# Interleaved first weight lists, a shorter layer-norm head and an epilogue inside the layer norm, in an eight-core decoder layer

## Chip, cores and metric

The kernel runs on all 8 cores of one Trainium2 chip (two dies of four cores), each core on 1024 tokens of its own; nothing is exchanged. The metric is device time in microseconds (us) of the slowest core. A program on all cores has a fast and a slow state: in many executions one die, or both, runs at a lower granted TensorE clock and the time grows by some per cent. Unless I say otherwise I compare executions in which no die was slowed ("fast"), or single dies at the full clock.

Ratios quoted as such are the mean time of one kernel's fast runs over the mean of the other's fast runs of the same rounds, so not quite the ratio of the medians or single times that I quote beside them.

## The reference

```python
D_MODEL, BATCH, SEQ, N_META = 4096, 4, 2048, 16
D_FF = 11008
def reference(x, meta_tokens, ...):
    h = concatenate([meta, x], axis=1)
    h = layer_norm(ALPHA * h + 0.5 * swiglu_ffn(h, ffn1...), ln1)
    h = layer_norm(ALPHA * h + hybrid_mixer(h, w_in, conv_w, pool_w, pool_scale, w_out), ln2)
    h = layer_norm(ALPHA * h + 0.5 * swiglu_ffn(h, ffn2...), ln3)
    return h[:, N_META:]
# layer_norm: mean and variance over the 4096 features, (x-mu)*rsqrt(var+1e-5)*g+b, in float32
# swiglu_ffn: silu(h Wg) * (h Wu), then Wd; hybrid_mixer: a projection to 8192 columns,
# a gated short convolution, four causal window means, an output projection
```

## The kernel before

Tokens lie along the free dimension, features along partitions, so the 4096 features are 32 chunks of 128. A core takes its tokens in two halves (528 columns, 16 of them a halo of earlier tokens, then 512). For each half it runs: prologue (load and transpose the input), FFN 1, layer norm, mixer, layer norm, FFN 2, layer norm, epilogue (transpose and store). `hacc` holds the residual in float32, `hb` the normalised activations in bf16.

Weights stream through a ring of five slots of 1 MB. One slot is one "unit": 16 chunks by 256 output columns, converted to bf16 on the way. A list of two units makes two banks of results in PSUM, where matmuls accumulate (four banks where the 528 columns are split in two):

```python
def mm_block(wv, col0, kchunks, rhs_fn, rhs_keys_fn, subs, b0):
    ...
    while k0 < nk_tot:
        nk = min(16, nk_tot - k0)
        slot = add_unit(wv, kchunks[0] + k0, nk, col0)     # DMA into ring[slot], waits until it is free
        ...                                                # fn: 16 x 2 matmuls (x nsub)
        reads = [("w", slot)]
        for kk in range(nk):
            reads += rhs_keys_fn(k0 + kk)                  # waits for all 16 chunks of hb
        P.op("pe", fn, reads=reads, writes=bkeys(b0, 2 * nsub))
```

The head of each layer norm, after ones-matmuls have summed over the partitions, and its loop:

```python
# ACT: mean = ps/D                        L349
# DVE: tmp = mean*mean                    L351
# DVE: tmp = ps2/D - tmp                  L353
# DVE: tmp = tmp + EPS                    L356
# ACT: tmp = Sqrt(tmp)                    L358
# DVE: rstd = 1/tmp                       L360
for c in range(NCH):
    # DVE: t1 = hacc[c] - mean            L366
    # DVE: t2 = t1 * rstd                 L368
    # not final: ACT hb[c], ACT hacc[c]   L376, L380
    # final:     ACT hacc[c]              L371
...
```

The epilogue came after that loop: for each block of 128 tokens, eight groups of four transposes, a copy of each group alternately on ACT and DVE into one of two staging buffers (16 KB in each partition), one 2 MB store. The prologue of the second half uses the same two buffers for its loads.

## Time and profile before

| | kernel before |
|---|---|
| first three timed runs | 9115.62, 9807.81, 10494.77 us (the first is fast) |
| profiled run, slowest core | 9118.2 us, clock 0.977, fast |
| PE busy | 8678.6 us, 95% |
| PE standing still | 440 us by subtraction; 394 us in the listed waits |

The lines themselves are in the prediction. Read them so: PE is the TensorE matmul row, ACT is ScalarE, DVE is VectorE, POOL issues the weight loads and SP the input loads and stores; a row of waits names the waiting engine and line, what it waited for, and then total us, number of waits and longest. A timeline row gives start, length, engine and line, output and inputs, count, and in brackets the idle time just before with what ended it. "PE ps L272 <- ACT hb L376" is the weight matmuls waiting for a chunk of `hb` that ACT writes at L376.

### The profile page before, as it was taken

Reading aid. Unit: us, or ns where it says so; the run is one execution under the profiler, and the core shown is the slowest. Engines: PE = TensorE matmul, PEld = TensorE weight load, DVE = VectorE, ACT = ScalarE, POOL = GpSimd, SP = SyncE. Lnnn points to the kernel's source line nnn. Section 1 sums busy time; section 2 is a strip of 40 time slices with the busy share of each in tenths; the row PEclk is TensorE's granted clock in tenths of the full one; section 3 lists DMA queues with packets and bytes.
Section 4 is the critical chain, followed back from the end, with each engine's and each line's share of the span. In section 5 each row is a group of like instructions: output and inputs, shape, how many; then the busy total and the mean of one; then the engine's idle time right before and its main releaser. Section 6 shows DMA issues by size and latency. Waiting matters only on the chain.

```text
span 9118.2 us, 110310 instructions; the slowest of 8 cores (9110.8 to 9118.2 us)
## 1 busy us (share of the span) xinstructions
PE 8678.6 (95%) x49081; PEld 4904.7 (54%) x49680; DVE 1259.2 (14%) x1482; ACT 646.0 (7%) x808; POOL 675.7 (7%) x1284
## 2 busy tenths in 40 slices
PE   8999999979989999999879999999799799999996
PEld 7888888867634444444444444444344344444443
DVE  1000000142130000000320000001412300000014
ACT  1000000020020000000120000000200200000002
POOL 0000000000000000000000000000000000000000
PEclk9999999989999999999989999999899899999998
DMA  8888888869878888898769898988698699998995
GB/s 156 147 145 148 144 150 146 145 104 154 146 126 140 150 155 153 151 154 151 138 152 154 150 155 150 155 152 149 111 159 146 115 152 151 154 153 150 155 150 111
DMA packets 187414, 1328.84 MB, mean 146 GB/s; under 512 B 20784, under 2 KB 21040, under 8 KB 47664
## 3 DMA queue, kind: packets, MB, share of 16 engines
q0 software_dynamic: 184320, 1287.73, 83.4%
q1 hardware_dynamic: 2624, 34.01, 1.1%
q8 instruction: 396, 6.49, 0.3%
q14 instruction: 74, 0.61, 0.0%
HBM read 2592.54 MB, written 16.78 MB: 286 GB/s over the span
## 4 chain that ended last, share of the span: by engine, by line
PE 94%; ACT 2%; DVE 2%; DMA 1%; issue 1%; DVEq 0%; ACTq 0%; SPq 0%
PE ps L272 93%; ACT hb L376 1%; DMA gy<-xin 1%; DVE scr L366 1%; ACT hacc L380 1%; PE ps L593 0%; DVE scr L368 0%; DMA y<-gy 0%; PE ps L339 0%; DVE scr L360 0%; PE ps L621 0%; DVE gy L630 0%; DVE scr L327 0%; ACT gy L627 0%; DVE scr L323 0%
## 5 line engine op out<-in xcount | busy, mean ns | idle before, releaser
L272 PE MATMUL ps<-hb,ring 128*128 128x512 bf16 (+1 forms) x32761 | 5702.1, 335 | 203.0 <-ACT hb L376 180.2
L272 PEld LDWEIGHTS ps<-hb,ring 128*128 128x128 bf16 x33152 | 3248.9, 98 | 2654.4 <-issue 203.2
L272 PE MATMUL ps<-gy,ring 128*128 128x512 bf16 (+1 forms) x15603 | 2838.8, 343 | 18.9 <-DVE gy L554 8.1
L272 PEld LDWEIGHTS ps<-gy,ring 128*128 128x128 bf16 x15808 | 1547.7, 98 | 1308.0 <-issue 14.5
L408 DVE TENSOR_TENSOR gy<-ps,scr 128x1024 bf16<-128x1024 f32 (+1 forms) x172 | 212.1, 1233 | 4587.9 <-PE ps L272 4587.9
L253 POOL DMA_DIRECT2D ring<-w_gu x688 | 363.2, 528 | 4687.9 <-PE ps L272 4641.3
L401 ACT ACTIVATE scr<-ps 128x1024 f32<-128x1024 f32 (+1 forms) x172 | 177.2, 1030 | 6149.2 <-PE ps L272 6149.1
L418 DVE SCALAR_TENSOR_TENSOR hacc<-ps,hacc 128x1024 f32<-128x1024 f32 (+1 forms) x192 | 236.8, 1233 | 1986.7 <-PE ps L272 1986.7
L253 POOL DMA_DIRECT2D ring<-w_d x384 | 202.6, 528 | 2250.9 <-PE ps L272 2216.5
L309 ACT ACTIVATE scr<-hacc 128x1024 f32<-128x1024 f32 (+1 forms) x96 | 101.9, 1062 | 1225.0 <-DVE hacc L418 775.0
L621 PE MATMUL ps<-identS,hacc 128*128 128x128 f32 x256 | 48.5, 345 | 103.2 <-ACT hacc L371 93.5
L368 DVE TENSOR_TENSOR scr<-scr 128x512 f32<-128x512 f32 (+1 forms) x192 | 133.5, 695 | 20.5 <-DVE scr L366 0.5
L253 POOL DMA_DIRECT2D ring<-w_in x128 | 67.5, 528 | 874.3 <-PE ps L272 865.2
L366 DVE TENSOR_TENSOR scr<-hacc,scr 128x512 f32<-128x512 f32 (+1 forms) x192 | 132.2, 688 | 0.6
L323 DVE TENSOR_TENSOR scr<-scr,hacc 128x512 f32<-128x512 f32 (+1 forms) x180 | 125.1, 695 | 21.2 <-DVE scr L323 1.4
L327 DVE TENSOR_TENSOR scr<-scr 128x512 f32<-128x512 f32 (+1 forms) x180 | 124.5, 691 | 9.4
L593 PE MATMUL ps<-identS,gy 128*128 128x128 f32 (+1 forms) x288 | 44.3, 330 | 73.7 <-DMA gy<-xin 73.6
L376 ACT ACTIVATE hb<-scr,vecsS 128x512 bf16<-128x512 f32 (+1 forms) x128 | 102.8, 803 | 20.8 <-DVE scr L368 20.7
L380 ACT ACTIVATE hacc<-scr,avecsS 128x512 f32<-128x512 f32 (+1 forms) x128 | 102.8, 803 | 0.0
L621 PEld LDWEIGHTS ps<-identS,hacc 128*128 128x128 f32 x256 | 37.6, 179 | 115.0 <-issue 114.5
L569 DVE TENSOR_TENSOR hacc<-ps,hacc 128x1024 f32<-128x1024 f32 x32 | 39.2, 1225 | 321.8 <-PE ps L272 321.8
L593 PEld LDWEIGHTS ps<-identS,gy 128*128 128x128 f32 (+1 forms) x288 | 43.0, 180 | 75.0 <-issue 75.0
(42 smaller groups left out, 584.1 us busy)
## 6 DMA issues: line engine op xcount, KB each, us to landing
ring<-w_gu POOLq DMA_DIRECT2D x688, 1024.0 KB, 9.1
ring<-w_d POOLq DMA_DIRECT2D x192, 1024.0 KB, 9.6
ring<-w_in POOLq DMA_DIRECT2D x128, 1024.0 KB, 9.5
ring<-w_d POOLq DMA_DIRECT2D x128, 768.0 KB, 8.1
ring<-w_out POOLq DMA_DIRECT2D x64, 1024.0 KB, 9.8
ring<-w_d POOLq DMA_DIRECT2D x64, 896.0 KB, 9.1
gy<-xin SPq DMA_DIRECT2D x8, 2048.0 KB, 17.2
y<-gy SPq DMA_DIRECT2D x8, 2048.0 KB, 8.1
```

Of the source, the lines that this page charges most:

```text
L253: return g.dma_start(out=dst, in_=src)
L272: inst = t.matmul(ps[:, b0 + c * nsub + si, 0:w], lhsT=ring[slot][:, kk, c * 128:(c + 1) * 128], rhs=rhs_fn(k0 + kk, si), start=(first and ...
L309: P.op("act", lambda a: a.activation(out=sq[:, :, c0:c0 + T], in_=hacc[:, ch:ch + 2, c0:c0 + T], func=AF.Square), reads=[("hacc", ch), ("h ...
L323: P.op("dve", lambda v, j=j: v.tensor_tensor(out=s1, in0=s1, in1=hacc[:, ch + j, c0:c0 + T], op=ALU.add), reads=[("hacc", ch + j)], writes ...
L327: P.op("dve", lambda v, j=j: v.tensor_tensor(out=s2, in0=s2, in1=sq[:, j, c0:c0 + T], op=ALU.add), reads=cells(C_SQ, 2), writes=cells(C_S2 ...
L366: P.op("dve", lambda v, t1=t1, hc=hc: v.tensor_tensor(out=t1, in0=hc, in1=mean, op=ALU.subtract), reads=[("hacc", c)] + cells(C_MEAN, 1), ...
L368: P.op("dve", lambda v, t1=t1, t2=t2: v.tensor_tensor(out=t2, in0=t1, in1=rstd, op=ALU.mult), reads=cells(C_T1[c % 2], 1) + cells(C_RSTD, ...
L376: P.op("act", lambda a, t2=t2, c=c: a.activation(out=hb[:, c, c0:c0 + T], in_=t2, func=AF.Identity, bias=vecs[:, vb + c:vb + c + 1], scale ...
L380: P.op("act", lambda a, t2=t2, hc=hc, c=c: a.activation(out=hc, in_=t2, func=AF.Identity, bias=avecs[:, vb + c:vb + c + 1], scale=avecs[:, ...
L401: P.op("act", lambda a, bg=bg, sgt=sgt: a.activation(out=sgt, in_=psv(bg, nsub, w), func=AF.Silu), reads=bkeys(bg, 2 * nsub), writes=cells ...
L408: P.op("dve", lambda v, bu=bu, sgt=sgt, gv=gv: v.tensor_tensor(out=gv, in0=psv(bu, nsub, w), in1=sgt, op=ALU.mult), reads=bkeys(bu, 2 * ns ...
L418: P.op("dve", lambda v, bd=bd, hv=hv: v.scalar_tensor_tensor(out=hv, in0=psv(bd, nsub, w), scalar=0.5, in1=hv, op0=ALU.mult, op1=ALU.add), ...
```

## The change

Three parts, meant to shrink the stretches where PE waits at the seams between stages:

1. **Interleaving.** A list becomes a sequence of grains of four chunks, and up to four lists (two in the first mixer, where a list takes four banks) run side by side while the layer norm still produces chunks.
2. **Head.** Square moves to ACT; Ln and Exp(-0.5 x) replace the addition of EPS, the square root and the reciprocal.
3. **Epilogue.** Transposes, copies and stores of the final layer norm go into its loop; a store is 1 MB of 512 columns of all 512 tokens.

The core of the diff (cut at the dots; here and below, remarks at the ends of lines are mine):

```diff
+        def run_interleaved(unit_lists):
+            half = len(unit_lists[0]) // 2
+            for i in range(half):
+                for u in unit_lists:
+                    u[i]()
+            for j, i in ((0, 0), (0, 1), (1, 0), (1, 1), (0, 2), (1, 2), (0, 3), (1, 3)):
+                unit_lists[j][half + i]()
+            for u in unit_lists[2:]:
+                for i in range(half, 2 * half):
+                    u[i]()
...
-            P.op("dve", lambda v: v.tensor_tensor(out=tmp, in0=mean, in1=mean, op=ALU.mult),
+            P.op("act", lambda a: a.activation(out=tmp2, in_=ps[:, b0:b0 + 2, 0:w2], func=AF.Square, scale=1.0 / D),
...
-            P.op("dve", lambda v: v.tensor_scalar_add(out=tmp, in0=tmp, scalar1=EPS),
-            P.op("act", lambda a: a.activation(out=tmp, in_=tmp, func=AF.Sqrt),
-            P.op("dve", lambda v: v.reciprocal(out=rstd, in_=tmp),
+            P.op("act", lambda a: a.activation(out=tmp, in_=tmp, func=AF.Ln, bias=epsc[:, 0:1]),
+            P.op("act", lambda a: a.activation(out=rstd, in_=tmp, func=AF.Exp, scale=-0.5),
...
+                ni = (2 if nsub == 1 else 1) if pi == 0 else 1      # FFN: two pairs = four lists, first group only
...
+            nz = 4 if ns1 == 1 else 2                               # mixer
+            zb = [alloc_banks(2 * ns1) for _ in range(nz)]
+            run_interleaved([z_units(i, zb[i], 4) for i in range(nz)])
...
+            def hook(c):                                            # called after chunk c of the final layer norm
+                g, j = c // 4, c % 4
+                if g > 0:
+                    copy(g - 1, j, "act")
+                    if j == 3:
+                        store(g - 1)
+                if j == 3:
+                    transposes(g)
+                if c == NCH - 1:
+                    for tb in range(4):
+                        copy(g, tb, "act" if tb % 2 == 0 else "dve")
+                    store(g)
...
-            ln_finish(V_LN + 128, V_LN + 160, off, 512, final=True)
-            epilogue(t, off)
+            ln_finish(V_LN + 128, V_LN + 160, off, 512, final=True, hook=epilogue(t, off))
```

## The prediction

> **What bounds the kernel now.** I read, in this order: the times and the cores, the page's busy shares and slices, the waits of PE, the PE timeline of one layer-norm seam and of the middle of the run, and the chain of work through one layer norm. All eight cores of the profiled run span 9110.8 to 9118.2 us at a granted clock of 0.977, so it is a fast run. The timed runs reach from 9115.62 to 10494.77, so the median of 9807.81 is a slow-state figure; I predict the fast state.
>
> From the page:
>
> ```profile
> PE 8678.6 (95%) x49081; PEld 4904.7 (54%) x49680; DVE 1259.2 (14%) x1482; ACT 646.0 (7%) x808; POOL 675.7 (7%) x1284
> ...
> PEclk9999999989999999999989999999899899999998
> DMA  8888888869878888898769898988698699998995
> ...
> HBM read 2592.54 MB, written 16.78 MB: 286 GB/s over the span
> ```
>
> PE is the bound: 95% busy, and in dense stretches (3000 to 3100 us) 99.5% at a clock of 1.00. The change removes no matmul, so all it can win lies in the 9118.2 - 8678.6 = 440 us when PE stands still, plus the slow matmuls after a pause. DMA at eight to nine tenths is a close second bound.
>
> The waits of PE, each with total us, times and longest:
>
> ```profile
> PE ps L272 <- ACT hb L376: 180.2, 8, 32.8
> PE ps L621 <- ACT hacc L371: 93.5, 16, 15.2
> PE ps L593 <- DMA gy<-xin: 73.6, 6, 22.7
> PE ps L339 <- DVE scr L327: 27.3, 6, 4.8
> ```
>
> The first row is four seams (layer norm into mixer, or into the second FFN, for both halves of the tokens) with two waits each. The second is the final layer norm, the third the input load, the fourth the end of the statistics. The change aims at the first two and half of the third.
>
> One seam on PE (start, length, instructions, idle before):
>
> ```profile
> 6446.82 3.54 PE L339 MATMUL ps<-scr,onesS 128*128 128x256 f32 x8 [4.47 <-DVE scr L327]
> 6482.49 9.56 PE L272 MATMUL ps<-hb,ring 128*128 128x512 bf16 x32 [32.13 <-ACT hb L376]
> 6505.06 1.87 PE L272 MATMUL ps<-hb,ring 128*128 128x512 bf16 x4 [13.01 <-ACT hb L376]
> ```
>
> One weight unit is 16 chunks, so PE waits for chunk 15, runs 32 matmuls, and waits for chunk 31. Chunks come every (6505.06 - 6482.49)/16 = 1.41 us; 32 warm matmuls take 6.9 us (32 x 0.2158, from 10.79 us per 50 in the chain). 45 us of idle are thus spent with one unit of work available.
>
> The head of a layer norm, from the chain:
>
> ```profile
> 4530.69 3.77 PE ps L339 x8
> ...
> 4534.54 0.60 ACT scr L349
> ...
> 4535.24 0.70 DVE scr L351
> ...
> 4536.10 0.70 DVE scr L353
> ...
> 4536.90 0.44 DVE scr L356
> ...
> 4537.41 1.28 ACT L358
> 4538.70 0.64 ACT scr L358
> ...
> 4539.43 3.36 DVE scr L360
> ...
> 4542.89 0.70 DVE scr L366
> ```
>
> 8.4 us of small serial steps, 3.36 of them one reciprocal.
>
> **What the Trainium skill says.** "ScalarE: Activation LUTs", section "Table sets: the hidden batching unit": exp and ln share the set natural_log_exp_and_others, so Ln followed by Exp needs one load. Its section "What ACT_TABLE_LOAD costs" gives 1283 ns for the load; the trace has four before Sqrt at 1283 ns mean, and no separate drain of that size between load and Sqrt (0.01 us). "TensorE: Matmul & The Clock Gate", "What's actually happening": after about 3.4 us of idle the clock falls to half until the array has been busy about as long. The trace agrees: the 32 matmuls after 32.13 us idle took 9.56 us instead of 6.9. "HBM Reference", "Specifications (TRN2)": about 358 GB/s per core when both cores of a pair stream; the trace shows 286 on average, and a lone weight unit landing in 8.7 us.
>
> **The change part by part.**
>
> *Head (all six layer norms).* Removed: multiply L351 (0.70), add L356 (0.44), reciprocal L360 (3.36). Square moves to ACT behind the mean, Ln takes Sqrt's place with its table load, Exp is new. By hand from the mean's start at 4534.54: mean and Square end at 4535.65, the DVE subtraction runs 4535.75 to 4536.45, load to 4537.8, Ln to 4538.5, Exp to 4539.15, first L366 at 4539.2 instead of 4542.89: 3.7 us earlier. If the order of the sets went wrong and Exp needed its own load, it would be 2.4.
>
> *Seams with 512 columns (mixer of the second half, second FFN of both).* Now four lists run together in grains of four chunks: 32 matmuls, 6.9 us of work, per 4 x 1.41 = 5.6 us of arrivals. So PE starts at chunk 3 and never catches up with the chunks. I compare the moment when all four lists (256 matmuls) are done. Before, at the seam shown: 6505.06 + 224 x 0.2158 + 2.2 for the cold start (9.56 and 8.99 us against 6.9 elsewhere) = 6555.6. After: start 6482.49 - 3.7 - 12 x 1.41 = 6461.9, plus 256 x 0.2158 + 2.2 = 57.4, is 6519.3. Won: 36.3. The same sum gives 36.2 at 2725.56/2748.11 and 35.6 at 7223.38/7245.56. Together 108.
>
> *Seam into the first mixer (264 columns, two lists).* A grain round is 32 x 0.113 = 3.6 us (28.96 us per 256 in the timeline) against 5.7 us of arrivals: PE waits in each round and ends one round after chunk 31. Before: 1993.76 + 192 x 0.1131 + 2.4 = 2017.9. After: 1993.76 - 3.7 + 3.6 = 1993.7, or about 2 later if the gaps leave the clock low. Won: 23.
>
> *Epilogue.* Transposes and copies go between the normalisations. DVE needs 1.40 us per chunk; ACT about 0.72 + 0.60 = 1.32 (spacing of L376/L380, duration of L627), so the loop should stay on DVE. Before, from the last normalisation at 9084.4 to the end at 9118.2: 33.8. After: 16 transposes (1.09 + 3 x 0.69 = 3.2), a copy 0.7, waits 0.3, a 1 MB store of about 5.2 (estimated from 6.6 to 7.4 for 2 MB) = 9.7. Won with the head: 24.1 + 3.7 = 27.8. In the middle:
>
> ```profile
> 4588.80 5.93 PE L621 MATMUL ps<-identS,hacc 128*128 128x128 f32 x32 [4.40 <-ACT hacc L371]
> ...
> 4634.11 8.84 PE L593 MATMUL ps<-identS,gy 128*128 128x128 f32 x64 [22.61 <-DMA gy<-xin]
> ...
> 4660.48 39.87 PE L272 MATMUL ps<-hb,ring 128*128 128x512 bf16 x181 [1.22 <-DVE hb L602]
> ```
>
> The first input load was issued at 4618.34, 29.6 us after the last normalisation (4588.7), behind the stores. After, it follows the last store issue: 4.6 us. The 42 us from there to the first weight matmul stay. Won: 25.0 + 3.7, less 1 for loads that now overlap more: 27.7.
>
> *Ring.* All five slots are held during the interleaved first halves, so DMA pauses and then has four units to fetch. The unit for list 1's second half is issued 5.2 us before the first halves end, lands 8.7 to 9.5 later, and is needed 3.45 after the end: up to 0.9 late, at four places (the interleaved start of the second half's first FFN included, which wins nothing): -3.6. Later units at 5.9 us each (estimated from the skill's 358 GB/s: 2.1 MB read per unit) gain about 1 us of margin per 6.9 us of PE work.
>
> Sum: 108 + 23 + 27.8 + 27.7 - 3.6 = 183 us. 9118 - 183 = 8935 us, a ratio of 0.980.
>
> **The rivals.** (1) The ring runs dry after each interleave. For it: DMA is at 0.89 to 0.96 in dense stretches and all cores refill together; the longest landing near the first mixer was 15.1 us. Against: a lone unit moves at about 200 GB/s where 150 are used. If a refill took over 6.9 us per unit, each of four places would lose 10 to 15 us: about 8985. (2) ACT becomes the bound in the final layer norm: with waits its identity and copy could take 0.81 + 0.60 + 0.15 = 1.56 per chunk instead of 1.40, 5 us a time: 8945. (3) The seam stays bound by arrivals with a cold PE: if the first rounds run at half clock beyond one window, 2 to 4 us at four seams: 8947. (4) A better case: the interleave saves a cold start more than I count, and the last store of 1 MB takes nearer 4 us than 5.2. For it speaks that each seam has two cold restarts before and one after; against it, that the second pause of 13 us left a smaller loss. Perhaps 8 us: 8925.
>
> **Range and chances.** The terms read off the trace (seams, head, epilogue) could each be off by a tenth, some 12 us together; the ring adds a tail upward only. Predicted 8936 us, 8 in 10 between 8910 and 8970. The 2% line lies at 0.98 x 9117 = 8934.7, all but on the prediction: faster by over 2% 0.48, within 2% 0.51, slower 0.01.
>
> **What would show it right or wrong.** Head: first L366-like subtraction 4.7 us after the statistics' matmuls, four loads before Ln, none before Exp. Seams: PE idle near 11 us once in place of 32 and 13, then a dense run; at the first mixer several gaps of about 2 us. Epilogue: last normalisation to end about 10 us, input load issued about 5 us after it. Ring: waits of PE on ring DMA absent or under 1 us each; waits of several us there would make the prediction too low. PE busy time should stay near 8670; if it grew, the clock was lower and the prediction wrong.

## The result, and the profile after

| | before | after |
|---|---|---|
| median of all runs | 9866.44 (15 runs) | 9690.76 (12 runs) |
| range | 9115.62 to 10679.78 | 8937.97 to 10742.02 |
| fast runs | 9115.62 to 9119.35 | 8937.97 to 8939.83 (5 of 12) |
| ratio of fast runs | | 0.9804, interval 0.979 to 0.9818 |

The fast runs lie 179 us under those of before, against a predicted 183; the interval straddles the line of 2%, so the verdict is unclear. The median of all executions is far outside the range, because 7 of the 12 were slow. The run that was profiled first was one of these, on both dies. From its page, the busy line and the granted clock in 40 slices:

```profile
PE 10290.1 (98%) x49680; PEld 5391.3 (51%) x49680; DVE 1213.7 (12%) x1437; ACT 665.8 (6%) x848; POOL 675.7 (6%) x1284
...
PEclk7888888878887888888878888888878878899999
```

PE is busy longer than the whole fast run lasts, with no matmul added, at granted clocks mostly in the seven and eight tenths. So I read the profile of a repetition (`after_again`) whose second die was undisturbed. Its view of the cores (span, mean granted clock):

```profile
core 5: 8937.7 us, clock 0.986
...
core 7: 8918.9 us, clock 0.987
die 0 (median of its cores): 9077.8 us, clock 0.969
die 1 (median of its cores): 8930.4 us, clock 0.987
```

The spans of the second die split: two cores near 8920 (cores 4 and 7), two near 8937 (5 and 6), at nearly the same clock. In all 28 dies of the changed kernel's executions that ran undisturbed (clock 0.975 or more on all four cores), exactly one core of each of the pairs 0-1, 2-3, 4-5 and 6-7 is the slower. In the kernel before, all eight cores of the profiled run were within 7.4 us. The slower core sets the time, so I take core 5, and core 7, a faster core of the other pair, beside it. The waits of PE on core 5:

```profile
PE ps L641 <- DMA gy<-xin: 63.3, 6, 22.1
PE ps L675 <- ACT hacc L393: 59.1, 16, 12.1
PE ps L279 <- ACT hb L399: 53.2, 9, 11.9
...
PE ps L279 <- DMA ring<-w_gu: 6.1, 3, 2.6
PE ps L279 <- DMA ring<-w_in: 1.8, 1, 1.8
```

Lines have moved: L279 is the old L272, L399 the old L376, L675 the epilogue's transposes, L641 the prologue's. The wait for `hb` fell from 180.2 to 53.2, that of the epilogue from 93.5 to 59.1, that for the input from 73.6 to 63.3, and a new wait of 7.9 us on the weight ring has come. On core 7 the last is 0.5, on core 4, the neighbour of core 5, 0.6, and on core 6 7.1.

The statistics matmuls (L339, now L363) end each stage, so the difference of two of their starts in the PE timeline is one stage with the seam at its head. The starts, in us from the start of the span:

| statistics matmuls | before, core 6 | after, core 5 | after, core 7 |
|---|---|---|---|
| first FFN, first half | 1934.45 | 1933.54 | 1931.16 |
| first mixer | 2690.94 | 2666.21 | 2663.88 |
| second FFN, first half | 4530.69 | 4470.89 | 4466.65 |
| first FFN, second half | 6446.82 | 6360.41 | 6348.74 |
| second mixer | 7188.14 | 7068.44 | 7053.51 |
| second FFN, second half | 9026.75 | 8873.55 | 8856.23 |
| end | 9118.2 | 8937.7 | 8918.9 |

What each stage became shorter by, against the predicted terms:

| stage | predicted | core 5 | core 7 |
|---|---|---|---|
| start to first statistics | 0 | 0.9 | 3.3 |
| first mixer | 23 | 23.8 | 23.8 |
| second FFN, first half | 36.2 | 35.1 | 37.0 |
| end of first half, input, first FFN | 27.7 | 26.6 | 34.0 |
| second mixer | 36.3 | 33.3 | 36.6 |
| second FFN, second half | 35.6 | 33.5 | 35.9 |
| last layer norm to the end | 27.8 | 27.3 | 28.8 |
| ring, not placed | -3.6 | (inside) | (inside) |
| sum | 183 | 180.5 | 199.3 |

The seam into the second mixer, on core 7 and on core 5 (PE timelines):

```profile
6348.74 3.75 PE L363 MATMUL ps<-scr,onesS 128*128 128x256 f32 x8 [4.82 <-DVE scr L351]
6364.22 57.55 PE L279 MATMUL ps<-hb,ring 128*128 128x512 bf16 x256 [11.73 <-ACT hb L399]
```

```profile
6360.41 3.55 PE L363 MATMUL ps<-scr,onesS 128*128 128x256 f32 x8 [4.82 <-DVE scr L351]
6375.70 33.89 PE L279 MATMUL ps<-hb,ring 128*128 128x512 bf16 x144 [11.74 <-ACT hb L399]
6411.41 24.33 PE L279 MATMUL ps<-hb,ring 128*128 128x512 bf16 x112 [1.81 <-DMA ring<-w_in]
```

Where before had idle 32.13 and 13.01, there is one of 11.7, and then all 256 matmuls of four lists without a gap: 57.55 us, 57.4 predicted. On core 5 the run breaks after 144 matmuls, just where the second unit of list 1 is wanted, and PE waits 1.81 us for it. That is the place that the prediction named.

The head, on all engines of core 5 at that seam:

```profile
6364.06 0.60 ACT L373 ACTIVATE scr<-ps 128x512 f32<-128x512 f32 x1 [5.99 <-PE ps L363]
...
6366.09 1.28 ACT L380 ACT_TABLE_LOAD   x1 [0.94 <-DVE scr L377]
6367.38 0.72 ACT L380 ACTIVATE scr<-scr,epsc 128x512 f32<-128x512 f32 x1
6368.20 0.63 ACT L382 ACTIVATE scr<-scr 128x512 f32<-128x512 f32 x1
6368.93 0.69 DVE L388 TENSOR_TENSOR scr<-hacc,scr 128x512 f32<-128x512 f32 x1 [2.92 <-ACT scr L382]
```

From the mean's start to the first subtraction is 6368.93 - 6364.06 = 4.87 us, before 4542.89 - 4534.54 = 8.35: 3.5 won, 3.7 predicted. There is one table load, before Ln, and none before Exp; the whole run has four of them, as before.

The stage between the halves, on PE of core 7:

```profile
4538.13 9.28 PE L641 MATMUL ps<-identS,gy 128*128 128x128 f32 x64 [14.46 <-DMA gy<-xin]
4552.39 8.84 PE L641 MATMUL ps<-identS,gy 128*128 128x128 f32 x64 [4.98 <-DMA gy<-xin]
4561.19 31.24 PE L279 MATMUL ps<-hb,ring 128*128 128x512 bf16 x144
4592.92 47.43 PE L279 MATMUL ps<-hb,ring 128*128 128x512 bf16 x219 [0.49 <-DMA ring<-w_gu]
```

The last transposes of the epilogue start at 4520.97 here, so the first weight matmul comes 40 us after them; before it came 72 us after the start of the 32 transposes at 4588.80. The first input load is issued at 4525.11, 4.1 us after them.

### The profile page after: what moved, and what is told of

Its sections match the earlier page's. It is cut to its first block, busy times and chain, and to the rows that moved or that the text cites. A ratio compares the mean times of both kernels' runs of the same rounds, so it can differ in the third digit from the quotient of the medians.

```text
span 10505.9 us, 110860 instructions; the slowest of 8 cores (10450.9 to 10505.9 us)
## 1 busy us (share of the span) xinstructions
PE 10290.1 (98%) x49680; PEld 5391.3 (51%) x49680; DVE 1213.7 (12%) x1437; ACT 665.8 (6%) x848; POOL 675.7 (6%) x1284
## 4 chain that ended last, share of the span: by engine, by line
PE 97%; DMA 1%; DVE 1%; ACT 1%; issue 0%; DVEq 0%; SPq 0%; ACTq 0%; POOLq 0%
PE ps L279 96%; DMA gy<-xin 1%; DVE scr L388 0%; PE ps L641 0%; DMA ring<-w_gu 0%; ACT hb L399 0%; PE ps L363 0%; DVE scr L390 0%; ACT hacc L403 0%; DVE scr L351 0%; DVE scr L347 0%; ACT L380 0%; DVE hacc L457 0%; PE ps L675 0%; ACT scr L380 0%
## 5 line engine op out<-in xcount | busy, mean ns | idle before, releaser
L279 PE MATMUL ps<-hb,ring 128*128 128x512 bf16 (+1 forms) x33152 | 6769.3, 377 | 52.2 <-ACT hb L399 51.0
L279 PEld LDWEIGHTS ps<-hb,ring 128*128 128x128 bf16 x33152 | 3570.9, 108 | 3248.6 <-issue 2469.0
L279 PE MATMUL ps<-gy,ring 128*128 128x512 bf16 (+1 forms) x15808 | 3371.8, 386 | 8.1 <-DVE gy L601 8.1
L279 PEld LDWEIGHTS ps<-gy,ring 128*128 128x128 bf16 x15808 | 1700.3, 108 | 1677.5 <-issue 1319.6
L641 PE MATMUL ps<-identS,gy 128*128 128x128 f32 (+1 forms) x288 | 48.1, 350 | 64.2 <-DMA gy<-xin 64.2
L675 PE MATMUL ps<-identS,hacc 128*128 128x128 f32 x256 | 49.6, 375 | 57.8 <-ACT hacc L393 57.8
L399 ACT ACTIVATE hb<-scr,vecsS 128x512 bf16<-128x512 f32 (+1 forms) x128 | 102.8, 803 | 7.0 <-DVE scr L390 6.8
L403 ACT ACTIVATE hacc<-scr,avecsS 128x512 f32<-128x512 f32 (+1 forms) x128 | 102.8, 803 | 0.0
L641 PEld LDWEIGHTS ps<-identS,gy 128*128 128x128 f32 (+1 forms) x288 | 46.6, 191 | 65.7 <-issue 65.7
L675 PEld LDWEIGHTS ps<-identS,hacc 128*128 128x128 f32 x256 | 44.6, 198 | 63.6 <-issue 63.6
```

Of the source, the lines that this page charges most:

```text
L279: inst = t.matmul(ps[:, b0 + c * nsub + si, 0:w], lhsT=ring[slot][:, kk, c * 128:(c + 1) * 128], rhs=rhs_fn(k0 + kk, si), start=(k0 + kk = ...
L399: P.op("act", lambda a, t2=t2, c=c: a.activation(out=hb[:, c, c0:c0 + T], in_=t2, func=AF.Identity, bias=vecs[:, vb + c:vb + c + 1], scale ...
L403: P.op("act", lambda a, t2=t2, hc=hc, c=c: a.activation(out=hc, in_=t2, func=AF.Identity, bias=avecs[:, vb + c:vb + c + 1], scale=avecs[:, ...
```

## The experiments

All twelve runs (nine different kernels) gave correct results. "Fast" counts executions without a slowed die. Each of the three sets ran on a chip of its own, with runs of the kernel before between them; its fast runs agree across the chips (9115.82 to 9121.08, 9117.12, 9117.33, and one at a lower clock, below).

| label | what it is | fast runs, us | against 9117 to 9118 |
|---|---|---|---|
| head_only | head alone | 9098.51 to 9099.32 (4 of 6) | -19 |
| interleave_only | interleaving alone | 9007.95, 9011.04 (2 of 8) | -108 |
| epilogue_only | epilogue alone | none of 8 | (dies: -48) |
| epilogue_b | the same again | 9069.47 (1 of 6) | -48 |
| after_again, after_b | the change again | 8936.51, 8936.71; 8939.79, 8940.85 | -179 |
| ring4 | the change, four slots | 8961.20 to 8963.01 (3 of 6) | -155 |
| stagger | the change, slot freed earlier | 8931.22 (1 of 6) | -186 |
| fine | small first grains | 8922.80, 8925.13 (and 8957.85 with a die at 0.983 to 0.985; 3 of 7) | -193 |
| input_mid | fine, input of half 2 early | 8907.45 (1 of 8) | -210 |
| input_early, best_b | the same, start reordered too | 8887.77 (and 8910.99, 8928.98; 3 of 8); 8887.10 (and 8963.22; 2 of 8) | -230 (the first of each) |

**after_again: the changed kernel once more.** No edit.

> The changed kernel once more, for a fast profile and for parts that share its runs of the kernel before. Theory (the predicted sum holds): fast runs at 8936 to 8940, 177 to 183 us under the kernel before; PE's waits for hb fall from 180 to about 55 us, those of the epilogue's transposes from 93 to 55 to 60, input load waits from 74 to about 64, waits for the weight ring under 4 us in total. Rival (two errors that cancel): the total is the same, but a term is off by more than 10 us in the three single-part runs.

Measured: 8936.51 and 8936.71, ratio 0.9789 with interval 0.9739 to 0.9839 (one of the runs of before that counted as fast had a die at 0.972 and took 9162.66, which widens it). The waits are shown above: 53.2, 59.1 and 63.3 as expected, but the ring took 7.9 us on the slower core, not under 4. The three single parts below decide against the rival: no part's total is off by more than 10 us.

**head_only.** The kernel before with the head lines of the diff alone.

> Kernel before plus the new head alone (Square on ScalarE, Ln and Exp for the square root and the reciprocal). Theory: six heads of 3.7 us, all on the path: 22 us less. Rival 1 (Exp takes its own table load): 14 us. Rival 2 (the head lies beside other work): under 5 us.

Measured: 9098.81, 9098.51, 9098.99, 9099.32; the median of before's fast runs in these rounds is 9118.09, so 19 us less. Six heads of 3.5 us are 21. Both rivals fall, 14 (a second table load) and under 5 (hidden): the four runs spread by under 1 us, and the fastest run of before, 9115.82, still lies 16.5 us above the slowest of them. The ratio: 0.9967.

**interleave_only.** The kernel before with `mm_units`, `run_interleaved` and their two uses alone.

> Kernel before plus the interleaved lists at four seams (and at the first FFN of the second half) alone. Theory: 3 x 32.5 + 19.3 - 3.6 for the ring = 113 us less. Rival (the ring runs dry after each interleave): 60 to 75 us less and waits of PE on ring DMA of 10 us and more in each place.

Measured: 9007.95 and 9011.04, 108 us less, against 113 expected and 60 to 75 for a dry ring. The split of the cores is there already: 8995.9, 9003.7, 8991.5, 9003.5 on die 0 of the first. In fast runs of head_only and epilogue_b the eight cores lie within 12 and 8 us of each other, without two groups, so the split belongs to the interleaving.

**epilogue_only, and epilogue_b.** The kernel before with `epilogue` as a hook of the final layer norm, and the 16 staging keys that go with it.

> Kernel before plus the new epilogue alone. Theory: 24 us at the end and 24 us in the middle, 48 us less. Rival (ScalarE becomes the bound in the final layer norm, 1.56 us per chunk instead of 1.40): about 38 us less, with the spacing of the normalisations at 1.5 to 1.6 us.

No execution of the first was fast. In five of the eight one die ran at the full clock; its cores took 9061.3 to 9066.8, where before's take 9107 to 9120.

> The new epilogue alone again, since no run of it was fast in both dies: undisturbed dies ran 9062 to 9067. Theory: a fast run at 9066 to 9070, 48 to 50 us under the kernel before. Rival (the undisturbed die gained because the other was slow, by having memory to itself): 9075 and over.

Measured: one fast run, 9069.47, 48 us under before. The waits of PE in that run, core 3:

```profile
PE ps L272 <- ACT hb L377: 180.2, 8, 32.8
PE ps L595 <- DMA gy<-xin: 66.0, 6, 23.2
PE ps L629 <- ACT hacc L371: 63.0, 16, 15.2
```

The seams' 180.2 is untouched to the tenth; the epilogue's wait and the input's are the large ones that moved. The groups of transposes in its last layer norm start 5.6 us apart (9054.12, 9059.72), that is 1.40 us per chunk as before: ScalarE did not become the bound. The undisturbed dies of the first attempt had told the same as the fast run. The three parts alone sum to 19 + 108 + 48 = 175, together they give 179; they hardly interact.

**ring4.** The changed kernel with

```diff
-NSLOT = 5
+NSLOT = 4
```

> The changed kernel with four weight slots instead of five. Theory (the ring is short only just after each interleaved start of four lists, and one core of each pair already loses about 8 us there): list 0's second half is no longer resident; it is issued 5.2 us before the first halves end and lands 3.7 us after, the next unit then 2.4 us late, so 6 us more at each of four places: 8960 to 8970 in fast runs, waits of PE on ring DMA of 25 to 35 us in total, none in dense stretches. Rival (the ring is not what separates the cores of a pair): under 5 us more.

Measured: 8961.20 to 8963.01, 24 us more than the changed kernel. Waits of PE on core 2, the slowest:

```profile
PE ps L279 <- DMA ring<-w_gu: 17.6, 5, 5.5
...
PE ps L279 <- DMA ring<-w_in: 2.2, 5, 0.8
```

Ten waits and 19.8 us instead of 7.9. One more hides under another name: at the second mixer the view has 5.79 us before the matmul at 6421.85 as "ACT hb L399", but the chunks that it needs were long written and a weight unit landed 0.25 us before it started. With it core 2 waited 25.6 us for the ring, as expected (25 to 35). On core 3 the named waits are 10.5 and two of the same kind ("ACT hacc L403", 3.27 and 3.18) make it 17.0, so the split persists. Six waits of core 2, 23.4 us, follow the four starts of four lists; the other five, 2.2 us together and 0.8 at most, lie in the two mixers. With about 49,000 weight matmuls in the run, four slots suffice nearly everywhere else.

**stagger.** The changed kernel with the order of grains altered, and no interleaving in the first FFN, which follows the prologue and has all chunks at once:

```diff
-            for i in range(half):
-                for u in unit_lists:
-                    u[i]()
+            if len(unit_lists) == 4:
+                for i in (0, 1):
+                    for u in unit_lists:
+                        u[i]()
+                for u in unit_lists:      # list 0 ends early, its slot is refilled early
+                    u[2]()
+                    u[3]()
...
-                ni = (2 if nsub == 1 else 1) if pi == 0 else 1
+                ni = 2 if (nsub == 1 and pi == 0 and li == 1) else 1
```

> The changed kernel with another order of the grains: the last two grains of each list's first half run list by list, so that slot 0 comes free about 5 us earlier, and the first FFN of the second half is not interleaved. Theory: the weight unit for list 1 lands in time, waits of PE on ring DMA fall under 1 us on all cores, the difference of about 15 us between the cores of a pair shrinks, slowest core 6 to 9 us lower: 8928 to 8931. Rival (the pair's difference comes from the input load or the stores): it stays above 10 us and the slowest core at 8934 to 8938.

Measured: one fast run, 8931.22, just above the range; the slowest core of the five undisturbed dies stands at 8925.6 (median), against 8935.7 in the 28 of the changed kernel. Waits on the ring have disappeared from the views of all eight cores, and the cores' spans are 8921.5, 8923.8, 8922.3, 8923.0, 8923.2, 8924.2, 8919.8, 8929.6. The seam, core 1:

```profile
6369.11 57.55 PE L279 MATMUL ps<-hb,ring 128*128 128x512 bf16 x256 [11.73 <-ACT hb L407]
```

The split of 15 us is gone with the ring waits: 2 to 10 us remain within an undisturbed die. So the interleaved starts made it, and the refill of the ring after them is the likely cause, but the edit changed two things at once. Nor are the waits the whole of it: cores 5 and 7 of the changed kernel lie 18.8 us apart, of which the ring waits are 7.4; another 7.4 is PE's busy time (8712.5 against 8705.1 for the same 49680 matmuls), the rest input and epilogue waits. How these come from the refill is not shown. Why one core of two neighbours loses and the other does not, is not shown either: which one it is changes from run to run (8934.9, 8918.8 and 8918.6, 8932.4 for cores 0 and 1 in two fast runs of the changed kernel), which fits two neighbours that refill at the same time and get in each other's way, but no run tried one core of a pair alone.

**fine.** The changed kernel with first-half grains of 1, 1, 2, 4, 4, 4 chunks, an order of the grains that frees slot 0 early, last grains of 4, 2, 1, 1 in the two-list seam, and `ni` as in stagger:

```diff
+FINE4 = ([1, 1, 2, 4, 4, 4], [4, 4, 4, 4])
+FINE2 = ([1, 1, 2, 4, 4, 4], [4, 4, 4, 2, 1, 1])
```

> As the changed kernel, with grains of 1, 1, 2, 4, 4, 4 chunks in the first halves, an order that frees slot 0 early, and grains down to one chunk at the end of the two-list seam. Theory (PE starts at chunk 0 and not 3, 4.2 us earlier, and gives back about 1.4 us waiting for chunks 23 and 31; the two-list seam ends 2.7 us earlier): 3 x 3 + 2.7 = 11 us less than the kernel with staggered order, 8916 to 8920. Rival (small grains cost in semaphore waits and cold matmuls what they win): no difference from the staggered order.

Measured: 8922.80 and 8925.13, 6 to 8 us under stagger's one fast run; by the slowest core of undisturbed dies 4 us (8921.6 against 8925.6, medians). Expected were 11: the sign is right, the size between a third and three quarters of it. The seam shows where the rest went, core 5:

```profile
6365.08 37.89 PE L287 MATMUL ps<-hb,ring 128*128 128x512 bf16 x160 [7.51 <-ACT hb L409]
6403.30 5.34 PE L287 MATMUL ps<-hb,ring 128*128 128x512 bf16 x24 [0.32 <-ACT hb L409]
6409.24 15.70 PE L287 MATMUL ps<-hb,ring 128*128 128x512 bf16 x72 [0.60 <-ACT hb L409]
```

PE starts after 7.51 us of idle instead of 11.73. But the first 160 matmuls take 37.89, 3.4 more than at the warm rate of 0.2158 us, where the whole of stagger's 256 take 2.3 more; and two waits, 0.92 us together, follow. Of 4.2 us, 2.1 arrive (the four lists end 70.8 us after the statistics' start, with stagger 72.9).

**input_early, and best_b.** As fine, and: scratch cells 0 to 7 serve as a third input buffer; the epilogue uses two of its four stages; the first two input blocks of the second half are loaded from the first chunk of the preceding final layer norm on; and at the start ring slots 1 to 4 wait for the fourth input block:

```diff
+               scr[:, 0:8, :].rearrange("p a n -> p (a n)")[:, 0:4096]]     # third STG
...
+        X_BUF = [[0, 1, 2, 0, 1], [1, 2, 0, 1]]
...
+                 extra_waits=[x_toks[0, 3]] if 1 <= ui < NSLOT else ())
...
+                if t == 0 and c == 0:                                          # in hook(c)
+                    x_load(1, 0, X_BUF[1][0])
+                    x_load(1, 1, X_BUF[1][1])
```

> As the fine-grained kernel, plus a third input buffer in scratch cells that are free then, the first two input blocks of the second half loaded during the final layer norm of the first, and at the start the ring's slots 1 to 4 loaded only after the fourth input block. Theory: the stage between the halves loses one of two serial load-and-transpose rounds, 11 us, and the start is bound by input bytes alone, first weight matmul at 45 to 50 us instead of 70: 8880 to 8890 in all. Rival (weights then come late at the start, so that PE waits for them instead): under 15 us won at the start.

Measured: 8887.77, and 8910.99 and 8928.98 in two more runs that count as fast, where some cores stood at 8909 or higher. PE of core 5, start and middle:

```profile
47.12 33.12 PE L289 MATMUL ps<-hb,ring 128*128 128x264 bf16 x293
...
4526.07 74.19 PE L289 MATMUL ps<-hb,ring 128*128 128x512 bf16 x343 [0.66 <-DVE hb L676]
```

The first weight matmul starts at 47.12 (50.51 on core 4) instead of 70.45, and PE does not wait for weights at the start. In the two slower runs, and in two slow ones (one of them of best_b), cores 6 and 7 stand together at 8908 to 8910 with a clock of 0.986 instead of 0.989 to 0.990; why, is open.

> The version with early input again, for a verdict against the kernel before from fast runs of the same rounds: 8886 to 8892 against 9117, ratio 0.975, faster by over 2%. Rival (the 8909 to 8929 seen on some dies at a barely lower clock are its true time): ratio 0.978 and over.

Measured: 8887.10, and 8963.22 in a run that counts as fast at a lower clock. Only one run of before was fast in these rounds (9117.33), so there is no interval; the single times give 8887.1 / 9117.33 = 0.975. The theory is supported, not closed: the expected 8886 to 8892 was met by one of the two runs, and the rival is not excluded.

**input_mid.** As input_early with `X_BUF[0] = [0, 1, 0, 1, 0]` and without `extra_waits`.

> As the version with early input, without its change at the start (two buffers, no delayed ring loads). Theory: of the about 36 us that it wins over the fine-grained kernel, the start is 20 to 23 (first weight matmul near 70 us instead of 47 to 51) and the middle the rest: 8908 to 8912. Rival (the middle wins nothing, since two rounds of loads remain behind the stores): 8920 and over.

Measured: one fast run, 8907.45. So of the 35 us from fine to input_early, 15 are the middle and 20 the start.

**after_b.** The changed kernel again.

> The changed kernel again, on a chip shared with the best version. Theory and rival as for its first repetition: fast runs at 8936 to 8940.

Measured: 8939.79 and 8940.85 in 8 executions, the second 0.85 above the expected range; the others were slow.

## Why the prediction was right or wrong

**The number, 8936 with a range of 8910 to 8970, does not hold the measured median of 9690.76.** The step that failed is the first paragraph's last clause: "I predict the fast state". The runs showed the slow state in 7 of 12 executions, at 9685.02 to 10742.02, so the median is a slow run; the five fast ones, 8937.97 to 8939.83, lie inside the range. The step was taken although two of the three runs known then were above 9800. In all, 9 of 28 executions of the changed kernel were fast, and 7 of 33 of the kernel before in the three sets of experiments. A figure for the median of an ordinary dozen of executions had to be some 2 to 11% above the fast time (the medians of these two kernels' sets are that much above), with a range of a thousand us. In both kernels most executions are slow, at clocks from 0.80 up; I draw nothing about the change from those. What puts a die into that state, no run tested. As a prediction of what the change does, step by step, it held:

- *PE is the bound and only its idle time can be won*: right. PE's busy time stays: with all 49680 records, 8713.4 on core 7 of the kernel before and 8712.5 on core 5 of the changed one. The 440 us and the 8670 of the prediction came from a core whose records are not all there; 397 us were to be won.
- *Head, 3.7 us*: 3.5 in the trace, 19 us for six alone. One table load, as reasoned from the set that Ln and Exp share.
- *Seams with 512 columns, 36 each*: 35.1, 33.3, 33.5 on core 5, 37.0, 36.6, 35.9 on core 7. The mechanism is right; most of core 5's shortfall is the ring wait at each of them, 1.8, 1.8 and 1.7.
- *First mixer, 23*: 23.8 on both. PE of core 7 waits there before its rounds as described, 1.7 and then 2.0 us (the second of these ends at 1964.03), and 0.3, 3.8 and 0.7 after that:

```profile
1946.79 9.76 PE L279 MATMUL ps<-hb,ring 128*128 128x264 bf16 x64 [11.93 <-ACT hb L399]
1958.29 3.76 PE L279 MATMUL ps<-hb,ring 128*128 128x264 bf16 x32 [1.73 <-ACT hb L399]
```

- *Epilogue at the end, 27.8*: 27.3. The sum of its parts was added wrongly (3.2 + 0.7 + 0.3 + 5.2 is 9.4, not 9.7); from the last normalisation to the end core 5 took 9.3. *In the middle, 27.7*: 26.6, but as two errors that cancel on core 5. "The 42 us from there to the first weight matmul stay" was wrong: from the first input load to the first weight matmul it took 4561.19 - 4525.11 = 36.1 on core 7 and 38.3 on core 5. Against that stood, on core 5, a ring wait of 2.6 in the same stage and about 2 us more in its later work that no wait explains. That 26.6 comes near 27.7 is partly luck.
- *Ring, -3.6*: mis-sized for the core that counts. It measured 7.9 on core 5 and 0.5 on core 7. I had taken "up to 0.9" at four places; the four waits are 1.7 to 2.6. The place was right, and so was the cause of the waits: stagger takes them away, ring4 enlarges them.
- *Rivals*: the dry ring (1) would have shown as 10 to 15 us at each place; it did not, even with four slots (7.3 at most). ACT as the bound (2) did not: 1.40 us per chunk. Cold rounds (3) cost nothing beyond the 2.2 counted. The better case (4), 8 us more, did not come: 179 us were won in all, against 183.
- *Chances*: 0.48 for faster by over 2% and 0.51 for within it. The ratio of 0.9804, with an interval across the line, is what they described.

## What to carry to other kernels

Where a matmul engine waits for a producer that delivers chunk by chunk, give it several independent lists to work on per chunk instead of one list with a coarse wait; the gain can be worked out from the trace as the matmuls done by the moment the last chunk lands. Then ask what the interleave holds: here all ring slots until the end of the first halves, which cost the slower core 8 us of waits until the order was changed so that one slot came free early. And say in which state of the chip a predicted number is meant, and what the mixture of states makes of a median, before giving a narrow range.

## What the Trainium skill lacked or had wrong

- "TensorE: Matmul & The Clock Gate", "Seeing it yourself", says that the peak-current limiter takes a die to 13/16 of the clock soon after a third core starts dense matmuls, and to budget for it in all-core kernels. Here all eight cores ran dense matmuls at a granted clock of 1.00 in fast runs (stretch 3000 to 3100 us), 16 of the 61 executions of the two kernels whose state is recorded (28 and 33) counted as fast, and the others had mean clocks of 0.80 to 0.97 on one die or both. The page does not say that it varies so from execution to execution.
- "ScalarE: Activation LUTs", "What ACT_TABLE_LOAD costs", adds a drain of about 1380 ns to the load's 1283 ns. The load measured 1283 ns; it began 0.08 us after the DVE result it waited for and the Ln began 0.01 us after it, so that no drain is to be seen there.
- "HBM Reference", "Specifications (TRN2)", gives equal shares of about 358 GB/s to two streaming cores. After the interleaved starts the neighbours did not fare alike: core 5 waited 7.9 us for the ring and core 4 0.6, and which core of a pair is the slower one changes between runs. Waits were measured here, not bandwidths. No page that I read has it, and its cause is open.
- No page that I read gives the cost of a finer wait between groups of matmuls. 32 waits per interleaved start with grains of four left the stream at 57.55 us for 256 matmuls, 2.3 over the warm rate, about what one cold start cost before (9.56 against 6.9 us at the seam shown), so the finer waits themselves cost next to nothing.
